# Longer input rows, a second state buffer and a new scheduling model in an eight-core hybrid decoder layer

## The chip, the cores and the metric

One Trainium2 chip, all eight cores, each working on its own 1120 token columns (1056 of a prompt, of which 32 are only history, and 64 of 16 sample sequences). The metric is the device time of the slowest core in microseconds (us). Some executions of these kernels fall into a slower state, in which the cores of one die show a lower granted clock: in a run of the changed kernel of 2220.78 us cores 4 to 7 had 0.818 to 0.819, the other four 0.988 to 0.991. Such runs are left out. I call a run undisturbed when all eight cores show a clock of 0.98 or more; this also leaves out some runs in which only a pair of cores was at 0.97 and about 20 us late.

## The reference, cut to what matters

```python
h = rmsnorm(x, norm_g); z = h @ w_in                 # one projection, split in 7 parts
u_a, gate_a, glu_val, glu_gate, gate_b, q, gate_c = jnp.split(z, splits, axis=-1)
o_a, new_pool = pool_mix(u_a, pool_state, ...)       # windowed means, x silu(gate_a)
a = glu_val * jax.nn.sigmoid(glu_gate)
o_b, new_conv = conv_module(a, conv_state, ...)      # depthwise conv of width 31, LayerNorm, swish, pointwise
o_c = memory_attention(q, mem_k, mem_v)              # 4 heads, 256 memory tokens, x silu(gate_c)
y = rmsnorm(x + concat([o_a, o_b, o_c]) @ w_out)     # returned with the new states
```

## The kernel before

The program is generated by Python code that keeps a model of every engine's time and orders the instructions by it. Weights come through a ring of nine units of 128x1024 in bf16 (GpSimd issues their loads). A projection block is 32 x 3 matmuls on four units; it accumulates in Z0 or Z1.

Start-up: x is loaded in pairs of tiles into three buffers, scaled into HT (bf16) and squared for the norm, while three blocks are accumulated.

```python
xT_d = din("xT", [32, 128, NT])                      # rows of 1120 f32, 4480 bytes
def x_load(a):
    S.dma("sp", ... out=XS[a % 3], in_=xT_d[2 * a:2 * a + 2].rearrange("b p n -> p b n") ...)
for a in range(16):
    act(... SQ2[a % 2] = Square(x_) ...)
    for i in range(2):
        dve(... HT[:, 2 * a + i, :] = x_[:, i, :] * g ...)
    if a:
        dve(... ACC += SQ2[a % 2] ...)
    if a + 3 < 16: x_load(a + 3)
    # ... 18 matmuls per pair; release(6, [HTk[27]]) after tile 27: six more weight units are issued
```

The sample sequences' convolution state of a block of 128 channels lies in ESA, a single buffer. A block's values are written into it, the convolution reads it, it is stored, and the next block's state is loaded.

```python
def v_mult(j, z, zb):
    flush_conv(conv_done, j - 2)
    flush_conv(conv_sampled, j - 1)                  # ESA of the block before is read and stored
    dve(... EA[b] = vp * sg ...)
    dve(... ESA[:, :, 30:34] = vs * sg ...)          # waits for the load; frees Z
```

Small steps of the attention (memory K/V units, scores, softmax, values) wait in a queue and are slipped between the units of the projections when the model says that their inputs are ready; `drain` forces those that are left at a deadline.

```python
def act(fn, n, r=(), w=(), wa=()):
    S.op("act", fn, r=r, w=w, wa=wa, cost=0.25 + n * 0.00084)
def slip():
    units = 0
    while small:
        _, r, w, run, need, un = small[0]
        if (need is not None and need not in given) or S.when("pe", r, w, 0.0) > S.t["pe"] - SLACK:
            break
        if un:
            if units == UNITS_AT_ONCE:
                break
            units += 1
        small.popleft(); run()
def gc_first(h):
    if h: drain(("p", h - 1))                        # values of head h-1 must be done
    gc_block(2 * h)
```

Of the kernel before, what the change touches and what calls it, by code (L numbers as in the profile page):

```python
# [15 lines left out]
D = 4096  # L16
# [7 lines left out]
PACE = 1.7  # L24
SLACK = 1.8
# [142 lines left out]
def build_program(loads=None):  # L168
# [8 lines left out]
    xT_d = din("xT", [32, 128, NT])  # L177
# [25 lines left out]
    with contextlib.ExitStack() as st:  # L203
# [91 lines left out]
        def act(fn, n, r=(), w=(), wa=()):  # L295
            S.op("act", fn, r=r, w=w, wa=wa, cost=0.25 + n * 0.00084)
# [13 lines left out]
        def slip():  # L310
            units = 0
            while small:
                _, r, w, run, need, un = small[0]
                if (need is not None and need not in given) or S.when("pe", r, w, 0.0) > S.t["pe"] - SLACK:
                    break
                if un:
                    if units == UNITS_AT_ONCE:
                        break
                    units += 1
                small.popleft()  # L320
                run()
# [39 lines left out]
        gets = [0]  # L361

        def unit(*key):
            k = gets[0]
            gets[0] += 1
            if recording:
# [6 lines left out]
        def release(n=1, after=()):  # L373
            stream["get"] += n
            fill(after)
# [9 lines left out]
        XS = [CCF[:, i * 2240:(i + 1) * 2240].rearrange("p (b n) -> p b n", b=2) for i in range(3)]  # L385
# [9 lines left out]
        def x_load(a):  # L395
            S.dma("sp", lambda e: e.dma_start(
                out=XS[a % 3], in_=xT_d[2 * a:2 * a + 2].rearrange("b p n -> p b n")), w=[XSb[a % 3]], kb=1120)

        for a in range(3):
            x_load(a)  # L400
        S.dma("act", lambda e: e.dma_start(out=ESA[:, :, :].rearrange("p a b -> p (a b)"), in_=sc_d[0]), w=[ESAb], kb=272)
# [8 lines left out]
        for a in range(16):  # L410
            x_, xb = XS[a % 3], XSb[a % 3]
            if a == 0:
# [3 lines left out]
            for i in range(2):  # L416
                kc = 2 * a + i
                dve(lambda e: e.tensor_scalar(out=HT[:, kc, :], in0=x_[:, i, :], scalar1=col(C_G + kc), scalar2=None,  # L418
                                              op0=ALU.mult), 560, r=[xb, CSb], w=[HTk[kc]])
            if a:  # L420
                dve(lambda e: e.tensor_tensor(out=ACC, in0=ACC, in1=SQ2[a % 2], op=ALU.add), 2240, r=[ACCb, SQ2b[a % 2]], w=[ACCb])  # L421
            if a + 3 < 16:
                x_load(a + 3)
            for i in range(2):
# [40 lines left out]
        act(lambda e: e.copy(out=SG[1][:, 1024:NT], in_=Z[0][:, 1120:1216]), 96, r=[Zb[0]], w=[SGb[1]])  # L465
        A0 = ACC[:, 0, :]
# [9 lines left out]
        def rb_sum(si):  # L476
# [4 lines left out]
                r=[mb], wa=[RBb])  # L481
# [49 lines left out]
        def win(s0, ns):  # L531
            base = ESA[:, s0:s0 + ns, :]
            return bass.AP(tensor=base.tensor, offset=base.offset, ap=[list(base.ap[0]), [34, ns], [1, 4], [1, 31]])

        def esa_load(j):
            S.dma("sp", lambda e: e.dma_start(out=ESA[:, :, :].rearrange("p a b -> p (a b)"), in_=sc_d[j]), w=[ESAb], kb=272)
# [8 lines left out]
        def push_conv(j):  # L545
# [3 lines left out]
            tmp = Y1[:, 0:992].rearrange("p (a t k) -> p a t k", a=8, t=4)  # L549

            def sampled():
                S.dma("act", lambda e: e.dma_start(out=css_d[j], in_=ESA[:, :, :].rearrange("p a b -> p (a b)")), r=[ESAb], kb=272)
                conv_sampled[0] = j
                if j + 1 < 12:
                    esa_load(j + 1)

            for s0 in (0, 8):
                piece(lambda e, s0=s0: e.tensor_tensor(
                    out=tmp, in0=win(s0, 8), in1=CS[:, wc:wc + 31][:, None, None, :].broadcast_to([128, 8, 4, 31]), op=ALU.mult),
                    992, r=[ESAb, CSb], w=[Y1b])  # L560
# [34 lines left out]
        def sigmoid_gate(sg, sgb):  # L595

            dve(lambda e: e.tensor_tensor(out=sg[:], in0=sg[:], in1=RB[:], op=ALU.mult), NT, r=[sgb, RBb], w=[sgb])
            act(lambda e: e.activation(out=sg[:], in_=sg[:], func=AF.Sigmoid), NT, r=[sgb], w=[sgb])
            dve(lambda e: e.tensor_tensor(out=sg[:], in0=sg[:], in1=RB[:], op=ALU.mult), NT, r=[sgb, RBb], w=[sgb])

        def gg_block(j):
# [3 lines left out]
            act(lambda e: e.activation(out=sg[:], in_=sg[:], func=AF.Sigmoid), NT, r=[sgb], w=[sgb])  # L605
            dve(lambda e: e.tensor_tensor(out=sg[:], in0=sg[:], in1=RB[:], op=ALU.mult), NT, r=[sgb, RBb], w=[sgb])

        def v_mult(j, z, zb):
# [3 lines left out]
            flush_conv(conv_sampled, j - 1)  # L612
# [764 lines left out]
```

## Time and profile before

| | before |
|---|---|
| time, median (all 15 runs of the first comparison) | 1911.7 us |
| TensorE busy on the slowest core | 1804.7 of 1908.7 us |
| start-up, until the block after it begins (mean of 8 cores) | 92.8 us |
| from there to the sum of the memory norm | 69.7 us |
| attention, gates, convolutions, to the pointwise stage | 788.7 us |
| the rest | 954.7 us |

The four stages are cut at instructions: the first matmul that waits for the copy of SG out of Z; the one-column matmuls PM<-ONES,PBT; the first multiply CC<-Z,SG on VectorE. In a view of waits the columns are the waiting engine and line, its releaser, the time in total, the times, the longest; in a timeline the start, the duration, engine, line, operation, and in brackets the idle time before it and its releaser. In the names, Z and PM are the accumulators of TensorE, HT the scaled input, SG, CC, G and EA work buffers on chip, RB the token norm, PBT the softmax's values, ring the weight units. In the kernel before L755 copies attention values out of PM, L733 writes the softmax, L803 multiplies memory values by their gate. "Cold" is said of matmuls at a low granted clock, "warm" of those at 1.00.

### The profile page before, as it was taken

How to read it: one execution, taken by the hardware profiler on the slowest of the kernel's cores; microseconds unless marked ns; L12 is line 12 of the kernel's file. 1: busy time of each engine (PE TensorE's matmuls, PEld its weight loads, DVE VectorE, ACT ScalarE, POOL GpSimd, SP SyncE). 2: the span in 40 equal slices, each digit the busy share in tenths (PEclk: the TensorE clock that was granted, in tenths of full speed). 3: DMA queues.
4: the chain of work that ended last, by engine and by line, in shares of the span. 5: the costliest groups of instructions: out<-in, count | busy, mean ns of one | idle time of the engine just before them, and what ended most of it. 6: DMA issues, size and time to landing. Idle time of an engine off the chain costs nothing.

```text
span 1908.7 us, 30037 instructions; the slowest of 8 cores (1901.3 to 1908.7 us)
## 1 busy us (share of the span) xinstructions
PE 1804.7 (95%) x11896; PEld 898.1 (47%) x11896; DVE 1045.5 (55%) x1056; ACT 295.4 (15%) x380; POOL 336.9 (18%) x630
## 2 busy tenths in 40 slices
PE   4799999999999999899999999999999999999991
PEld 2344454544445544455444444444444444444461
DVE  4878989877999998864622222333311111111168
ACT  2542141301113111151400000000000000000010
POOL 1112222122112211222111111111121111111121
PEclk9999999999999999999999999999999999999996
DMA  9986978789757754677375545454687556555559
GB/s 242 260 169 101 159 128 133 126 130 159 136 84 120 115 95 81 101 121 113 61 137 89 84 77 83 77 83 77 103 142 155 116 107 120 107 106 108 106 163 319
DMA packets 129066, 238.28 MB, mean 125 GB/s; under 512 B 19008, under 2 KB 39968, under 8 KB 128416
## 3 DMA queue, kind: packets, MB, share of 16 engines
q0 software_dynamic: 87680, 158.31, 54.5%
q1 hardware_dynamic: 33184, 68.88, 10.9%
q10 hardware_dynamic: 8064, 9.18, 1.4%
q8 instruction: 96, 1.57, 0.3%
q14 instruction: 42, 0.34, 0.1%
HBM read 357.47 MB, written 31.54 MB: 204 GB/s over the span
## 4 chain that ended last, share of the span: by engine, by line
PE 75%; DVE 9%; issue 7%; DMA 5%; ACT 3%; DVEq 0%; ACTq 0%; SPq 0%; POOL 0%; POOLq 0%
PE Z L299 72%; PE PM L299 4%; DMA CC<-xT 3%; DVE CC L572 2%; DMA ring<-w_in 1%; DVE Y L576 1%; ACT PM L728 1%; DVE HT L1201 1%; ACT CC L415 1%; DVE CC L561 0%; DVE SM L723 0%; ACT L728 0%; DVE CC L1201 0%; DVE G L781 0%; DVE SG L781 0%
## 5 line engine op out<-in xcount | busy, mean ns | idle before, releaser
L299 PE MATMUL Z<-HT,ring 128*128 128x512 bf16 (+1 forms) x7232 | 1158.2, 320 | 46.6 <-DVE HT L418 32.0
L299 PEld LDWEIGHTS Z<-HT,ring 128*128 128x128 bf16 x7232 | 562.5, 98 | 629.8 <-issue 70.8
L299 PE MATMUL Z<-CC,ring 128*128 128x512 bf16 (+4 forms) x3336 | 513.6, 317 | 1.9 <-DVE QS L1140 1.7
L299 PEld LDWEIGHTS Z<-CC,ring 128*128 128x128 bf16 x3336 | 254.2, 98 | 260.3 <-issue 2.5
L359 POOL DMA_DIRECT2D ring<-w_in x304 | 162.1, 535 | 778.1 <-PE Z L299 644.4
L572 DVE SCALAR_TENSOR_TENSOR CC<-EA,CS,CC 128x1024 f32<-128x1024 f32 x180 | 230.0, 1278 | 0.3 <-DVE RM L674 0.3
L576 DVE SCALAR_TENSOR_TENSOR Y<-EA,CS,Y 128x1024 f32<-128x1024 f32 x168 | 214.6, 1277 | 0.0
L359 POOL DMA_DIRECT2D ring<-w_out x121 | 64.0, 529 | 382.6 <-PE Z L299 363.8
L1140 DVE TENSOR_TENSOR HT<-Z,EA 128x1088 f32<-128x1088 f32 x16 | 20.7, 1292 | 172.4 <-PE Z L299 172.4
L1022 DVE TENSOR_TENSOR EA<-Z,RB 128x1056 f32<-128x1056 f32 x12 | 15.1, 1258 | 118.0 <-PE Z L299 118.0
L299 PE MATMUL PM<-ring,CC 128*128 128x512 bf16 x256 | 59.7, 379 | 0.0
L781 DVE TENSOR_TENSOR G<-Z,RB 128x1088 f32<-128x1088 f32 x16 | 20.5, 1283 | 63.7 <-PE Z L299 63.7
L1144 DVE TENSOR_TENSOR SS<-SS,SG 128x1088 f32<-128x1088 f32 x27 | 34.9, 1293 | 37.0 <-ACT SG L1142 37.0
L1142 ACT ACTIVATE SG<-HT 128x1088 f32<-128x1088 f32 x16 | 17.8, 1111 | 218.1 <-DVE HT L1140 218.1
L782 ACT ACTIVATE SG<-SG 128x1088 f32<-128x1088 f32 x8 | 8.9, 1112 | 261.6 <-DVE SG L781 261.6
L781 DVE TENSOR_TENSOR SG<-Z,RB 128x1088 f32<-128x1088 f32 x8 | 10.3, 1292 | 69.8 <-PE Z L299 69.8
L782 ACT ACTIVATE G<-G 128x1088 f32<-128x1088 f32 x16 | 17.8, 1111 | 195.8 <-DVE G L781 195.7
L421 DVE TENSOR_TENSOR CC<-CC 128x2240 f32<-128x2240 f32 x15 | 37.3, 2487 | 5.0 <-ACT CC L415 5.0
L415 ACT ACTIVATE CC<-CC 128x2240 f32<-128x2240 f32 x15 | 31.1, 2073 | 41.3 <-DMA CC<-xT 38.6
L299 PEld LDWEIGHTS PM<-ring,CC 128*128 128x128 bf16 x256 | 23.4, 98 | 27.0
L418 DVE TENSOR_SCALAR HT<-CC,CS 128x1120 bf16<-128x1120 f32 x32 | 24.2, 798 | 19.2 <-DMA CC<-xT 19.1
L782 ACT ACT_TABLE_LOAD x13 | 16.7, 1283 | 110.6 <-DVE G L781 66.5
(185 smaller groups left out, 987.9 us busy)
## 6 DMA issues: line engine op xcount, KB each, us to landing
ring<-w_in POOLq DMA_DIRECT2D x304, 256.0 KB, 4.8
ring<-w_out POOLq DMA_DIRECT2D x121, 256.0 KB, 3.9
CC<-xT SPq DMA_DIRECT2D x16, 1120.0 KB, 11.5
EA<-xT SPq DMA_DIRECT2D x28, 544.0 KB, 4.6
ring<-w_mem_k POOLq DMA_DIRECT2D x32, 256.0 KB, 5.9
ring<-w_mem_v POOLq DMA_DIRECT2D x32, 256.0 KB, 6.1
ring<-ckT POOLq DMA_DIRECT2D x32, 256.0 KB, 5.2
ring<-cvP POOLq DMA_DIRECT2D x32, 256.0 KB, 4.9
```

The costliest lines, as they stand in the source:

```text
L299: S.op("pe", lambda e: e.matmul(out, lhsT=lhsT, rhs=rhs, start=start, stop=stop, skip_group_check=skip), r=r, w=w, inc=inc, cost=max(0.05, ...
L359: S.dma("pool", lambda e: e.dma_start(out=RING[s][:, 0:n], in_=src), r=after, w=[RINGb[s]])
L415: act(lambda e: e.activation(out=SQ2[a % 2], in_=x_, func=AF.Square), 2240, r=[xb], w=[SQ2b[a % 2]])
L418: dve(lambda e: e.tensor_scalar(out=HT[:, kc, :], in0=x_[:, i, :], scalar1=col(C_G + kc), scalar2=None, op0=ALU.mult), 560, r=[xb, CSb], w ...
L421: dve(lambda e: e.tensor_tensor(out=ACC, in0=ACC, in1=SQ2[a % 2], op=ALU.add), 2240, r=[ACCb, SQ2b[a % 2]], w=[ACCb])
L572: piece(lambda e, k=k: e.scalar_tensor_tensor(out=YB[j][:, 0:NP_], in0=EA[b][:, 2 + k:2 + k + NP_], scalar=col(wc + k), in1=YB[j][:, 0:NP_ ...
L576: piece(lambda e, k=k: e.scalar_tensor_tensor(out=Y1[:, 0:NP_], in0=EA[b][:, 2 + k:2 + k + NP_], scalar=col(wc + k), in1=Y1[:, 0:NP_], op0 ...
L728: act(lambda e: e.activation(out=m[0:rows, t * 256:(t + 1) * 256], in_=m[0:rows, t * 256:(t + 1) * 256], func=AF.Exp, scale=1.0 / 16, bias ...
L781: dve(lambda e: e.tensor_tensor(out=g[:, 0:W], in0=z[:, 0:W], in1=RB[:, 32:NT], op=ALU.mult), W, r=[zb, RBb], w=gb)
L782: act(lambda e: e.activation(out=g[:, 0:W], in_=g[:, 0:W], func=AF.Silu), W, r=gb, w=gb)
L1140: dve(lambda e: e.tensor_tensor(out=yv, in0=z[:, 0:W], in1=XR[db % 2][:], op=ALU.add), W, r=[zb, XRb[db % 2]], w=[yb])
L1144: dve(lambda e: e.tensor_tensor(out=SY[:], in0=SY[:], in1=SQo[:, 0:W], op=ALU.add), W, r=[SYb, SQob], w=[SYb])
```

## The change

Its intent: load x faster, share the start-up's work with ScalarE, take the wait for the one ESA buffer away at the first block, and let the scheduling model know of table loads and of the supply of weights.

```diff
+UNIT_US = 1.85
-    xT_d = din("xT", [32, 128, NT])
+    xT_d = din("xT", [16, 128, 2 * NT])             # one row of 8960 bytes per pair
+        def act(fn, n, r=(), w=(), wa=(), tab=None):
+            load = tab is not None and tab != table[0]
+            if load:
+                table[0] = tab
+            S.op("act", ..., cost=0.25 + n * 0.00084 + (1.3 if load else 0.0))
 def slip():
-    ... S.when("pe", r, w, 0.0) > S.t["pe"] - SLACK:
+    ... S.when("pe", r, w, 0.0) > S.t["pe"] - (1.2 if small[0][0] == ("rb",) else SLACK):
-                    if units == UNITS_AT_ONCE:
+                    if units == UNITS_AT_ONCE or landed[gets[0] + 1] > S.t["pe"] - 0.5:
 def unit(*key):
+            S.t["pe"] = max(S.t["pe"], landed[k])
 def release(n=1, after=()):
+            for _ in range(n):
+                landed.append(max(landed[-1], S.t["pe"] + 2.2) + UNIT_US)
 for a in range(16):
+            dve(... HT[:, 2 * a, :] = x_[:, 0, :] * g ...)
+            act(... HT[:, 2 * a + 1, :] = Copy(x_[:, 1, :], scale=g) ...)
+            if a > 1:
+                x_sum(a - 1)                        # the sum, one pair later
             act(... Square ...)
-            (both scalings and the sum on VectorE)
+            if a == 13:
+                esa_load(0)                         # was issued at the start
+                esa_load(1)                         # into G[0]
+        def esa(j): G[0] for j == 1, otherwise ESA
-            flush_conv(conv_sampled, j - 1)
+            flush_conv(conv_sampled, j - 1 if j > 2 else j - 2)
 def gc_first(h):
+            else:
+                flush_conv(conv_sampled, 1)
-    ... qs[3] + sp_[3:4] + gs[2] + sp_[4:5] + gs[3]
+    ... qs[3] + gs[2] + sp_[3:5] + gs[3]
 # cut: tab="..." at the calls with a table function, the later reads of xT, the host's layout of xT
```

More of the change, by code (lines that the diff above doesn't have):

```diff
@@ L293, in dve @@
             dve_raw(fn, n, r, w, wa)
-        def act(fn, n, r=(), w=(), wa=()):
-            S.op("act", fn, r=r, w=w, wa=wa, cost=0.25 + n * 0.00084)
+        table = [None]
+        def act(fn, n, r=(), w=(), wa=(), tab=None):
+            load = tab is not None and tab != table[0]
+            if load:
+                table[0] = tab
+            S.op("act", fn, r=r, w=w, wa=wa, cost=0.25 + n * 0.00084 + (1.3 if load else 0.0))
         def mm(out, lhsT, rhs, start, stop, n, r, w, inc=True, skip=False):
@@ L313, in slip @@
                 _, r, w, run, need, un = small[0]
-                if (need is not None and need not in given) or S.when("pe", r, w, 0.0) > S.t["pe"] - SLACK:
+                if (need is not None and need not in given) or S.when("pe", r, w, 0.0) > S.t["pe"] - (1.2 if small[0][0] == ("rb",) else SLACK):
                     break
                 if un:
-                    if units == UNITS_AT_ONCE:
+                    if units == UNITS_AT_ONCE or landed[gets[0] + 1] > S.t["pe"] - 0.5:
                         break
@@ L361, in build_program @@
         gets = [0]
+        landed = [0.0] * NRING
         def unit(*key):
@@ L384, in build_program @@
         fill()
-        XS = [CCF[:, i * 2240:(i + 1) * 2240].rearrange("p (b n) -> p b n", b=2) for i in range(3)]
+        XSF = [CCF[:, i * 2240:(i + 1) * 2240] for i in range(3)]
+        XS = [t.rearrange("p (b n) -> p b n", b=2) for t in XSF]
         XSb = [Buf("XS%d" % i) for i in range(3)]
@@ L395, in x_load, with x_sum, esa, esa_load @@
         def x_load(a):
-            S.dma("sp", lambda e: e.dma_start(
-                out=XS[a % 3], in_=xT_d[2 * a:2 * a + 2].rearrange("b p n -> p b n")), w=[XSb[a % 3]], kb=1120)
+            S.dma("sp", lambda e: e.dma_start(out=XSF[a % 3], in_=xT_d[a]), w=[XSb[a % 3]], kb=1120)
+        def x_sum(a):
+            dve(lambda e: e.tensor_tensor(out=ACC, in0=ACC, in1=SQ2[a % 2], op=ALU.add), 2240, r=[ACCb, SQ2b[a % 2]], w=[ACCb])
+        def esa(j):
+            if j == 1:
+                return G[0][:, 0:544].rearrange("p (s r) -> p s r", s=16), G[0][:, 0:544], Gb[0]
+            return ESA[:, :, :], ESA[:, :, :].rearrange("p a b -> p (a b)"), ESAb
+        def esa_load(j):
+            _, t, tb = esa(j)
+            S.dma("sp", lambda e: e.dma_start(out=t, in_=sc_d[j]), w=[tb], kb=272)
         for a in range(3):
             x_load(a)
-        S.dma("act", lambda e: e.dma_start(out=ESA[:, :, :].rearrange("p a b -> p (a b)"), in_=sc_d[0]), w=[ESAb], kb=272)
         act(lambda e: e.copy(out=IDB[:], in_=IDF[:]), 128, r=[IDb], wa=[IDb])
@@ L411, in build_program @@
             x_, xb = XS[a % 3], XSb[a % 3]
+            dve(lambda e: e.tensor_scalar(out=HT[:, 2 * a, :], in0=x_[:, 0, :], scalar1=col(C_G + 2 * a), scalar2=None,
+                                          op0=ALU.mult), 560, r=[xb, CSb], w=[HTk[2 * a]])
+            act(lambda e: e.activation(out=HT[:, 2 * a + 1, :], in_=x_[:, 1, :], func=AF.Copy, scale=col(C_G + 2 * a + 1)), NT,
+                r=[xb, CSb], w=[HTk[2 * a + 1]])
+            if a > 1:
+                x_sum(a - 1)
             if a == 0:
@@ L415, in build_program @@
                 act(lambda e: e.activation(out=SQ2[a % 2], in_=x_, func=AF.Square), 2240, r=[xb], w=[SQ2b[a % 2]])
-            for i in range(2):
-                kc = 2 * a + i
-                dve(lambda e: e.tensor_scalar(out=HT[:, kc, :], in0=x_[:, i, :], scalar1=col(C_G + kc), scalar2=None,
-                                              op0=ALU.mult), 560, r=[xb, CSb], w=[HTk[kc]])
-            if a:
-                dve(lambda e: e.tensor_tensor(out=ACC, in0=ACC, in1=SQ2[a % 2], op=ALU.add), 2240, r=[ACCb, SQ2b[a % 2]], w=[ACCb])
             if a + 3 < 16:
                 x_load(a + 3)
+            if a == 13:
+                esa_load(0)
+                esa_load(1)
             for i in range(2):
@@ L465, in build_program @@
         act(lambda e: e.copy(out=SG[1][:, 1024:NT], in_=Z[0][:, 1120:1216]), 96, r=[Zb[0]], w=[SGb[1]])
+        x_sum(15)
         A0 = ACC[:, 0, :]
@@ L480, in rb_sum @@
             act(lambda e: e.activation(out=RB[:, c0:c1], in_=m[:, 0:c1 - c0], func=AF.Sqrt, scale=1.0 / D, bias=EPS), c1 - c0,
-                r=[mb], wa=[RBb])
+                r=[mb], wa=[RBb], tab="sqrt")
             recip(RB[:, c0:c1], c1 - c0, RBb)
@@ L529, in flush_conv, with win @@
                 convq.popleft()[1]()
-        def win(s0, ns):
-            base = ESA[:, s0:s0 + ns, :]
+        def win(j, s0, ns):
+            base = esa(j)[0][:, s0:s0 + ns, :]
             return bass.AP(tensor=base.tensor, offset=base.offset, ap=[list(base.ap[0]), [34, ns], [1, 4], [1, 31]])
-        def esa_load(j):
-            S.dma("sp", lambda e: e.dma_start(out=ESA[:, :, :].rearrange("p a b -> p (a b)"), in_=sc_d[j]), w=[ESAb], kb=272)
         def piece(fn, n, r=(), w=(), wa=(), after=None, first=False):
@@ L549, in push_conv @@
             tmp = Y1[:, 0:992].rearrange("p (a t k) -> p a t k", a=8, t=4)
+            _, es, esb = esa(j)
             def sampled():
-                S.dma("act", lambda e: e.dma_start(out=css_d[j], in_=ESA[:, :, :].rearrange("p a b -> p (a b)")), r=[ESAb], kb=272)
+                S.dma("act", lambda e: e.dma_start(out=css_d[j], in_=es), r=[esb], kb=272)
                 conv_sampled[0] = j
-                if j + 1 < 12:
-                    esa_load(j + 1)
+                nxt = 2 if j == 0 else j + 1
+                if j != 1 and nxt < 12:
+                    esa_load(nxt)
             for s0 in (0, 8):
                 piece(lambda e, s0=s0: e.tensor_tensor(
-                    out=tmp, in0=win(s0, 8), in1=CS[:, wc:wc + 31][:, None, None, :].broadcast_to([128, 8, 4, 31]), op=ALU.mult),
-                    992, r=[ESAb, CSb], w=[Y1b])
+                    out=tmp, in0=win(j, s0, 8), in1=CS[:, wc:wc + 31][:, None, None, :].broadcast_to([128, 8, 4, 31]), op=ALU.mult),
+                    992, r=[esb, CSb], w=[Y1b])
                 piece(lambda e, s0=s0: e.tensor_reduce(
@@ L597, in sigmoid_gate @@
             dve(lambda e: e.tensor_tensor(out=sg[:], in0=sg[:], in1=RB[:], op=ALU.mult), NT, r=[sgb, RBb], w=[sgb])
-            act(lambda e: e.activation(out=sg[:], in_=sg[:], func=AF.Sigmoid), NT, r=[sgb], w=[sgb])
+            act(lambda e: e.activation(out=sg[:], in_=sg[:], func=AF.Sigmoid), NT, r=[sgb], w=[sgb], tab="sig")
             dve(lambda e: e.tensor_tensor(out=sg[:], in0=sg[:], in1=RB[:], op=ALU.mult), NT, r=[sgb, RBb], w=[sgb])
@@ L604, in gg_block @@
             dve(lambda e: e.tensor_tensor(out=sg[:], in0=z[:, 0:NT], in1=RB[:], op=ALU.mult), NT, r=[zb, RBb], w=[sgb])
-            act(lambda e: e.activation(out=sg[:], in_=sg[:], func=AF.Sigmoid), NT, r=[sgb], w=[sgb])
+            act(lambda e: e.activation(out=sg[:], in_=sg[:], func=AF.Sigmoid), NT, r=[sgb], w=[sgb], tab="sig")
             dve(lambda e: e.tensor_tensor(out=sg[:], in0=sg[:], in1=RB[:], op=ALU.mult), NT, r=[sgb, RBb], w=[sgb])
@@ L611, in v_mult @@
             flush_conv(conv_done, j - 2)
-            flush_conv(conv_sampled, j - 1)
+            flush_conv(conv_sampled, j - 1 if j > 2 else j - 2)
+            ev, _, evb = esa(j)
             if z is None:
-                vp, vs, vb = EA[b][:, 0:1056], ESA[:, :, 30:34], [EAb[b], ESAb]
+                vp, vs, vb = EA[b][:, 0:1056], ev[:, :, 30:34], [EAb[b], evb]
             else:
@@ L618, in v_mult @@
                 r=vb + [sgb], w=[EAb[b]])
-            dve(lambda e: e.tensor_tensor(out=ESA[:, :, 30:34], in0=vs, in1=sg[:, 1056:NT].rearrange("p (s r) -> p s r", s=16),
-                                          op=ALU.mult), 64, r=vb + [sgb], wa=[ESAb])
+            dve(lambda e: e.tensor_tensor(out=ev[:, :, 30:34], in0=vs, in1=sg[:, 1056:NT].rearrange("p (s r) -> p s r", s=16),
+                                          op=ALU.mult), 64, r=vb + [sgb], wa=[evb])
             S.dma("act", lambda e: e.dma_start(out=csp_d[j], in_=EA[b][:, 1026:1056]), r=[EAb[b]], kb=16)
@@ L672, in mem_sum @@
                        [IDb, PBb[0]], [PMb[1]], inc=(i == 1))
-            act(lambda e: e.activation(out=RM[:, 0:2], in_=PM[1][:, 0:2], func=AF.Sqrt, scale=1.0 / D, bias=EPS), 2, r=[PMb[1]], w=[RMb])
+            act(lambda e: e.activation(out=RM[:, 0:2], in_=PM[1][:, 0:2], func=AF.Sqrt, scale=1.0 / D, bias=EPS), 2, r=[PMb[1]], w=[RMb], tab="sqrt")
             dve(lambda e: e.reciprocal(out=RM[:, 0:2], in_=RM[:, 0:2]), 12, r=[RMb], wa=[RMb])
@@ L729, in softmax @@
                                            scale=1.0 / 16, bias=sm[0:rows, 4 + t:5 + t], accum_out=sm[0:rows, 8 + t:9 + t]), 256,
-                    r=[mb, smb], wa=[mb, smb])
+                    r=[mb, smb], wa=[mb, smb], tab="exp")
             dve(lambda e: e.reciprocal(out=sm[0:rows, 12:12 + ng], in_=sm[0:rows, 8:8 + ng]), 12, r=[smb], wa=[smb])
@@ L781, in gate @@
             dve(lambda e: e.tensor_tensor(out=g[:, 0:W], in0=z[:, 0:W], in1=RB[:, 32:NT], op=ALU.mult), W, r=[zb, RBb], w=gb)
-            act(lambda e: e.activation(out=g[:, 0:W], in_=g[:, 0:W], func=AF.Silu), W, r=gb, w=gb)
+            act(lambda e: e.activation(out=g[:, 0:W], in_=g[:, 0:W], func=AF.Silu), W, r=gb, w=gb, tab="silu")
         def gc_block(c):
@@ L910, in ln_stat @@
                 r=[PMb[1], ESAb], wa=[QSb])
-            act(lambda e: e.activation(out=va, in_=va, func=AF.Sqrt, scale=1.0, bias=EPS), n, r=[QSb], wa=[QSb])
+            act(lambda e: e.activation(out=va, in_=va, func=AF.Sqrt, scale=1.0, bias=EPS), n, r=[QSb], wa=[QSb], tab="sqrt")
             recip(va, n, QSb)
@@ L921, in swish @@
                     act(lambda e: e.activation(out=CC[:, 2 * j, :], in_=YB[j], func=AF.Silu, scale=col(C_LNG + j), bias=col(C_LNB + j)),
-                        W, r=[yb[0], CSb], w=yb)
+                        W, r=[yb[0], CSb], w=yb, tab="silu")
                 piece(lambda e, j=j: e.tensor_tensor(out=YB[j], in0=YB[j], in1=SS[:], op=ALU.subtract), W, r=[SSb, yb[0]], w=yb)
@@ L936, in build_program @@
         sp_ = [lambda i=i: gb_spill(i) for i in range(5)]
-        others.extend(qs[0] + qs[1] + gs[0] + sp_[0:1] + qs[2] + sp_[1:2] + gs[1] + sp_[2:3] + qs[3] + sp_[3:4] + gs[2] + sp_[4:5] + gs[3])
+        others.extend(qs[0] + qs[1] + gs[0] + sp_[0:1] + qs[2] + sp_[1:2] + gs[1] + sp_[2:3] + qs[3] + gs[2] + sp_[3:5] + gs[3])
         others.extend(lambda dj=dj: gb_block(dj) for dj in range(7))
@@ L1127, in xr_load @@
             if db < NFULL:
-                S.dma("sp", lambda e: e.dma_start(out=XR[db % 2][:], in_=xT_d[db][:, 32:NT]), w=[XRb[db % 2]], kb=544)
+                S.dma("sp", lambda e: e.dma_start(out=XR[db % 2][:], in_=xT_d[db // 2][:, (db % 2) * NT + 32:(db % 2 + 1) * NT]), w=[XRb[db % 2]], kb=544)
         xr_load(0)
@@ L1188, in xq_load @@
                 t, tb = XQ[i % 4]
-                S.dma("pool", lambda e: e.dma_start(out=t[:, 0:c1 - c0], in_=xT_d[NFULL + r][:, 32 + c0:32 + c1]), w=[tb],
+                S.dma("pool", lambda e: e.dma_start(out=t[:, 0:c1 - c0], in_=xT_d[(NFULL + r) // 2][:, (r % 2) * NT + 32 + c0:(r % 2) * NT + 32 + c1]), w=[tb],
                       kb=(c1 - c0) / 2)
@@ L1208, in seg_sum @@
             ones_mm(m[:, 0:n], mb, HLs[0][:, 0:n], HLs[1][:, 0:n], HLsb)
-            act(lambda e: e.activation(out=SY[:, c0:c1], in_=m[:, 0:n], func=AF.Sqrt, scale=1.0 / D, bias=EPS), n, r=[mb], wa=[SYs[si]])
+            act(lambda e: e.activation(out=SY[:, c0:c1], in_=m[:, 0:n], func=AF.Sqrt, scale=1.0 / D, bias=EPS), n, r=[mb], wa=[SYs[si]], tab="sqrt")
             recip(SY[:, c0:c1], n, SYs[si])
@@ L1334, in _host_inputs @@
         m = dict(shared)
-        m.update({"xT": np.ascontiguousarray(x.T).reshape(32, 128, NT), "memT": memT[b],
+        m.update({"xT": np.ascontiguousarray(x.T.reshape(16, 2, 128, NT).transpose(0, 2, 1, 3)).reshape(16, 128, 2 * NT), "memT": memT[b],
                   "ckT": np.ascontiguousarray(ckc).reshape(4, 8, 128, 1024),
```

## The prediction

Passages that told of the hardware what no trace of this case shows are cut out of the prediction, and the cuts are marked. Its sum came to 24 us: 7.5 for parts 1 to 3, 6.5 for the second buffer, 10 for the scheduling model. The 7.5 is the 9.3 us of parts 1 to 3 less 1.8 us that I took off for a limit of the memory (HBM) and for waits for weights, an estimate of mine that no trace shows. The 331 GB/s are read in 20 to 40 us of core 3; what limit they should be held against is not shown, so the rival that the memory limits the start-up has little for it. The 1.28 us are a load of a function table on ScalarE.

> **What bounds the kernel now**
>
> I read the table of cores first. All eight lie between 1901 and 1909 us at clocks of 0.984 to 0.988, so the profiled run is an undisturbed one (1909.74 us), and one core (core 3) can stand for all. Then the page: busy time and slices.
>
> ```profile
> PE 1804.7 (95%) x11896; PEld 898.1 (47%) x11896; DVE 1045.5 (55%) x1056; ACT 295.4 (15%) x380; POOL 336.9 (18%) x630
> PE   4799999999999999899999999999999999999991
> DMA  9986978789757754677375545454687556555559
> ```
>
> TensorE is busy 95% of the span. The change leaves its matmuls alone, so it can only win what TensorE loses: 104 us of idle time plus time at a low clock. The windows say where the idle lies: 58 - 29.3 = 28.7 us before 58, 7.4 us in 58 to 90, 4 us around 125, 9 us in 280 to 420, 8.7 us in 420 to 830, 39 us after 1860, little elsewhere. The tail and the pure matmul stages are not touched. Next, who TensorE waited for:
>
> ```profile
> PE Z L299 <- DVE HT L418: 32.0, 13, 13.5
> PE Z L299 <- DMA ring<-w_in: 6.6, 4, 4.8
> PE PM L299 <- ACT CC L755: 6.2, 7, 1.5
> PE Z L299 <- DVE ESA L619: 4.1, 1, 4.1
> ...
> PE PM L752 <- ACT PBT L733: 3.4, 2, 3.1
> PE PM L299 <- DVE CC L803: 2.8, 2, 1.4
> ```
>
> The first line is the start-up (x loaded, scaled into HT, three blocks accumulated meanwhile). VectorE is named because it writes HT, but its own timeline shows two regimes: until about 58 us it waits for x, after that it never rests, and a pair of x tiles takes 3.83 us:
>
> ```profile
> 38.93 1.52 DVE L418 TENSOR_SCALAR HT<-CC,CS 128x1120 bf16<-128x1120 f32 x2 [1.76 <-DMA CC<-xT]
> ...
> 75.31 1.51 DVE L418 TENSOR_SCALAR HT<-CC,CS 128x1120 bf16<-128x1120 f32 x2
> 76.73 2.48 DVE L421 TENSOR_TENSOR CC<-CC 128x2240 f32<-128x2240 f32 x1
> 79.14 1.51 DVE L418 TENSOR_SCALAR HT<-CC,CS 128x1120 bf16<-128x1120 f32 x2
> ```
>
> The DMA queues in three windows, columns packets, MB, share of the 16 engines. First 12 to 20 us (x and weights), then 58 to 66 (x alone), then 100 to 118 (the memory tokens, 8192-byte rows, and weights):
>
> ```profile
> q1 hardware_dynamic: 322, 1.37, 58.8%
> q0 software_dynamic: 322, 0.59, 44.9%
> ```
>
> ```profile
> q1 hardware_dynamic: 544, 2.30, 98.0%
> ```
>
> ```profile
> q0 software_dynamic: 721, 1.31, 50.4%
> q1 hardware_dynamic: 398, 2.87, 48.4%
> ```
>
> So the engines are full from 2 us to the end of the loads even with x alone, at only 288 GB/s, and x and the weights take turns one packet each. Loads of x landed about 6.6 us apart while weights came too (12.5, 19.4, 25.9, 32.5, 39.0), about 3.8 us apart later.
>
> After start-up:
>
> ```profile
> 128.04 36.67 PE L299 MATMUL Z<-HT,ring 128*128 128x512 bf16 x216 [4.12 <-DVE ESA L619]
> ...
> 396.30 0.26 PE L752 MATMUL PM<-IDB,PBT 64*128 64x64 bf16 x2 [3.10 <-ACT PBT L733]
> ...
> 802.86 5.33 PE L299 MATMUL Z<-HT,ring 128*128 128x512 bf16 x24 [4.84 <-DMA ring<-w_in]
> ```
>
> The chain behind the first: ESA's store issued at 118.43, its next load at 123.89, landed by 127.57, then the multiply that frees Z. The third follows a burst of eight units drained together at 796.3, which emptied the weight ring.
>
> [...]
>
> - [...] 322 packets against 322. Longer x packets thus win a larger share against the weights.
> - [...] 3.81 MB of x and 1.41 MB of weights, which are read at twice that size as f32, are 6.63 MB in 20 us, 331 GB/s. [...]
> - [...] after the 4.12 us gap the granted clock is 0.58 in 126 to 130 and 0.57 in 130 to 134, then 1.00. [...]
> - [...] The trace shows 1.28 us; the old scheduling model charged none.
>
> **The change part by part**
>
> *1. x in rows of 8960 bytes instead of two of 4480.* From 58 to 66 us: 2.30 MB are 513 packets of 4480 bytes, 0.98 x 8 us x 16 / 513 = 244 ns each. From 100 to 118 us, 350 packets of 8192 bytes took 0.484 x 18 x 16 / 350 = 398 ns each. The slope is 154 ns per 3712 bytes, the fixed part about 58 ns; an 8960-byte packet is then estimated at 430 ns against 488 for two. Each engine carries 128 fewer packets: 128 x 58 ns = 7.4 us. Since the engines are full all along, that comes off the landing of the last x tile (84.9 us)[...]. Taking turns with a weight packet of 189 ns, a load of x needs 8 x (430 + 189) = 4.95 us instead of 16 x (244 + 189) = 6.9. The first nine weight units are 81 packets per engine and now last to about 2 + 81 x 0.62 = 52 us; the set for tile 16 is wanted at about 48, so TensorE waits for weights there, but has time to catch up (2.8 us of work per pair against 3.4 to 5 of loading).
>
> *2. The first ESA load moves behind the x loads.* 8 packets per engine, about 1 us off the start. In return the six weight units released after tile 27 come earlier against the last load and take turns with its 8 packets: 8 x 189 ns = 1.5 us, of which about 0.5 was paid before. The two cancel.
>
> *3. ScalarE scales every second HT tile; the sum is put off by one pair.* VectorE falls from 3.83 to 0.72 + 2.40 = 3.1 us a pair, ScalarE rises to 1.1 + 2.07 = 3.2. Both lie below the 3.44 us of a load (8 x 430 ns), so the DMA alone paces the end. VectorE lagged the landings by 1.9 us (84.91 landed, 86.79 scaled); that lag goes. Parts 1 to 3: 7.4 + 1.9 = 9.3 us at most. [...]
>
> *4. A second buffer (G0) for ESA of block 1.* The multiply needs neither store nor load. It can run after the gate's last multiply (ends 120.98): 1.25 + 0.23, done at 122.5 in today's times, 1.4 us before TensorE asks (123.92). The 4.1 us go, and the cold stretch, 5.4 us at 0.57 to 0.58, gives about 2.4 more: 6.5. G0 is first wanted at 246.8 and the conv pieces that read it end at 198, so the added flush costs nothing.
>
> *5. The scheduling model.* It now charges 1.3 us per table load, models when a weight unit lands, and takes a small unit only if the next weight will be there; two spilled gates move between the third and fourth group of memory gates, so the units drained at 796 can slip in earlier. At stake after 140 us: ring 5.3, L755 6.2, L733 3.4, L803 2.8, and some 3 us at a low clock (24 matmuls took 5.33 and 5.43 us where 3.85 is usual): about 20. The two long waits are what is modelled; I expect both gone (8 us and 3 of clock), a third of the short ones saved, and about 4 us returned as new waits from slower draining: 10 us net.
>
> Sum: 7.5 + 6.5 + 10 = 24 us, 1910.5 - 24 = 1886.5.
>
> **Rivals**
>
> - *The start is limited by HBM, not per packet.* For it: the mixed stage already reads 331 GB/s. Against: x alone ran at 288 with full engines. Then only the 1.9 us lag and little else is won: about 1892.
> - *ScalarE becomes the pace.* 3.2 us a pair plus waits is close to 3.44, and it now frees a buffer 3.2 us after a landing instead of 2.1. With two loads still in flight I think it hidden; otherwise 1 to 3 us are lost.
> - *Slower pacing collects units that must be drained at the deadlines.* It would show as bursts and new ring waits; part 5 gives 0 to 3: about 1894.
> - *Everything works and small waits vanish too:* 9.3 + 7 + 18 = 34 us, 1876.
>
> **Range and chances**
>
> A gain over 2% means under 1872.3, thus 38 us, more than the sum of all upper ends (9.3 + 7 + 20 = 36): 5%. Slower by 2% would need a broken schedule: 1%. The parts are nearly independent, with errors of some 3, 1.5 and 5 us; I widen that to a range of 1876 to 1898.
>
> **What the profile will show**
>
> Right, if: x loads in packets of 8960 bytes at about 430 ns, the last landing at 77 to 79 us and the matmuls after start-up beginning at 83 to 86 (before: 92.2); VectorE waiting for x up to the end; no wait on ESA near 118 and full clock there; no wait of TensorE over 2 us between 140 and 1000; later stages as before, shifted. Wrong, if: x packets take 480 ns or more, ScalarE has no gaps from 50 to 80 us, or waits for the ring or new drains appear. Matmuls and the tail from 1860 should cost the same; a shift there would mean that I missed something.

## The result, and the profile after

The changed kernel took 1877.98 us in the median of 11 runs against 1911.7. The ratio is 0.9825 (95% interval 0.9815 to 0.9834). It is the mean time of one kernel's runs over that of the other's of the same rounds, so not quite the ratio of the medians. Executions in which one die ran at a lower clock are left out of the means. The gain of 33.7 us lies in the predicted range and within 2%, but near the lower end of the range (1876 to 1898 us): 24 us were expected.

| mean of 8 cores, us | start-up | to the memory norm | attention and conv | rest | end |
|---|---|---|---|---|---|
| before | 92.8 | 69.7 | 788.7 | 954.7 | 1905.8 |
| after | 87.1 | 64.7 | 766.5 | 953.9 | 1872.2 |
| difference | -5.7 | -5.0 | -22.2 | -0.8 | -33.6 |

The page of the changed kernel, busy time and slices of TensorE:

```profile
PE 1796.6 (96%) x11896; PEld 897.1 (48%) x11896; DVE 1036.0 (55%) x1040; ACT 312.4 (17%) x395; POOL 336.8 (18%) x630
PE   4799999999999999999999999999999999999991
```

The matmuls are the same and take 8 us less busy time, so less of it was at a low clock; the one slice with an 8 is gone. Who TensorE waited for (slowest core, core 3 as before):

```profile
PE Z L306 <- DMA ring<-w_in: 22.4, 5, 14.8
PE PM L306 <- DMA ring<-w_in: 6.9, 3, 4.4
PE Z L306 <- DVE HT L437: 6.9, 6, 2.0
PE PM L306 <- DVE SG L1296: 3.7, 1, 3.7
```

The waits on the evacuations by ScalarE (L755, L733), on CC L803 and on ESA have no counterpart. The waits for the ring grew, but all of that growth lies in start-up (25.1 us of the 29.3; after 100 us they are 4.3, against 5.3 before), where they stand for what was called a wait for HT before: TensorE now has x before it has weights. Its timeline shows this, and where the start-up ends (92.21 in the kernel before):

```profile
14.85 1.09 PE L306 MATMUL Z<-HT,ring 128*128 128x512 bf16 x3 [14.85 <-DMA ring<-w_in]
...
24.74 1.01 PE L306 MATMUL PM<-HT,ring 128*128 128x512 bf16 x2 [4.40 <-DMA ring<-w_in]
...
87.22 7.75 PE L306 MATMUL Z<-HT,ring 128*128 128x512 bf16 x48 [1.47 <-ACT SG L493]
```

The DMA queues of the changed kernel in 12 to 20 us (x and weights):

```profile
q1 hardware_dynamic: 217, 1.69, 69.9%
q0 software_dynamic: 223, 0.40, 31.5%
```

Still one packet each, but x now gets 1.69 MB in this stretch instead of 1.37, and the weights 0.40 instead of 0.59. In 66 to 74 us x is nearly alone:

```profile
q1 hardware_dynamic: 308, 2.47, 93.7%
```

These 2.47 MB are 276 packets of 8960 bytes (the other 32 packets have 4 bytes and take about 9 ns), which took 0.937 x 8 x 16 / 276 = 435 ns each. The prediction set an estimated 430 ns against 2 x 244 ns, measured in one window of core 3. The packet records of all cores, over the whole loading of x, say less: 437 ns in the mean for a long packet, and 230 ns for a short one, so 460 ns for two. The other half of the comparison was off, not the estimate.

Around the former ESA wait, windows of TensorE (busy time, count, granted clock, DMA share, GB/s), before:

```profile
126.00:130.00 4.00, 1.96 (x7) 0.58 0.64 112
130.00:134.00 4.00, 4.00 (x17) 0.57 0.00 0
```

and after:

```profile
118.00:122.00 4.00, 4.00 (x28) 1.00 0.40 58
122.00:126.00 4.00, 4.00 (x28) 1.00 0.66 92
126.00:130.00 4.00, 4.00 (x28) 1.00 0.78 211
130.00:134.00 4.00, 4.00 (x28) 1.00 0.90 184
```

There is no gap, so there are no cold matmuls after it: 28 matmuls in each 4 us, against 7 and 17. (The changed kernel is 5 us earlier here, so the place of the old wait lies in the first two windows.)

### The profile page after: what moved, and what is told of

Its sections match the earlier page's. It is cut to its first block, busy times and chain, and to the rows that moved or that the text cites. A ratio compares the mean times of both kernels' runs of the same rounds, so it can differ in the third digit from the quotient of the medians.

```text
span 1876.8 us, 30032 instructions; the slowest of 8 cores (1868.5 to 1876.8 us)
## 1 busy us (share of the span) xinstructions
PE 1796.6 (96%) x11896; PEld 897.1 (48%) x11896; DVE 1036.0 (55%) x1040; ACT 312.4 (17%) x395; POOL 336.8 (18%) x630
## 4 chain that ended last, share of the span: by engine, by line
PE 90%; DMA 5%; DVE 3%; ACT 1%; issue 1%; DVEq 0%; SPq 0%; POOL 0%; ACTq 0%; POOLq 0%
PE Z L306 86%; PE PM L306 4%; DMA CC<-xT 3%; DMA ring<-w_in 1%; DVE HT L1232 1%; DVE CC L1232 0%; ACT CC L446 0%; DVE G L810 0%; DVE SG L810 0%; PE PM L781 0%; DVE SS L489 0%; DVE G L1232 0%; ACT CC L444 0%; ACT HT L439 0%; DVE QS L1171 0%
## 5 line engine op out<-in xcount | busy, mean ns | idle before, releaser
L367 POOL DMA_DIRECT2D ring<-cvP x32 | 17.0, 530 | 83.8 <-PE Z L306 34.5
L367 POOL DMA_DIRECT2D ring<-ckT x32 | 17.4, 545 | 75.9 <-PE PM L306 45.6
```

The source lines that it names most:

```text
L367: S.dma("pool", lambda e: e.dma_start(out=RING[s][:, 0:n], in_=src), r=after, w=[RINGb[s]])
```

## The experiments

The question left by the result: which parts carry the 22 us of the third stage, of which I had expected 10, and why start-up gave less. My theory was that the parts add up. The rivals were that the scheduling gains come from the other parts shifting the program against its small steps, and that within the scheduling part a single piece does it. Every kernel here gave correct results. The first four ran on a chip on which a pair of cores often lagged, in runs of the kernel before too, so their ratios are blurred; I compare undisturbed runs and the stages. The stages are of the profiled run of each kernel, the time is the median of its undisturbed runs.

| kernel | time, us | start-up | to memory norm | attention, conv | ratio to before (95%) |
|---|---|---|---|---|---|
| after (first set) | 1877.3 | 87.1 | 64.7 | 766.5 | 0.9825 (0.9815-0.9834) |
| s_none | 1902.0 | 88.1 | 64.7 | 789.3 | 0.9917 (0.9876-0.9958) |
| b_sched | 1887.3 | 92.9 | 71.3 | 769.9 | 0.9863 (0.9807-0.9919) |
| e_one | 1883.7 | 87.9 | 72.4 | 769.7 | 0.9855 (0.9778-0.9932) |
| s_table | 1896.9 | 87.4 | 64.7 | 785.9 | 0.9951 (0.9882-1.0021) |
| s_landed | 1878.9 | 87.5 | 64.7 | 766.7 | 0.9850 (0.9815-0.9886) |
| s_order | 1885.2 | 87.1 | 64.7 | 772.7 | 0.9859 (0.9846-0.9871) |
| x_rows | 1881.8 | 90.6 | 64.7 | 765.8 | 0.9860 (0.9831-0.9888) |
| x_split | 1879.4 | 88.3 | 64.7 | 767.8 | 0.9830 (0.9817-0.9842) |
| after_again | 1877.3 | 87.1 | 64.7 | 766.8 | 0.9820 (0.9808-0.9833) |
| x_xs4 | 1875.7 | 86.4 | 64.7 | 766.2 | 0.9814 (0.9802-0.9827) |
| x_xs4_late | 1876.3 | 86.8 | 64.7 | 766.3 | 0.9816 (0.9804-0.9829) |
| best | 1887.7 | 86.8 | 64.7 | 785.4 | 0.9877 (0.9860-0.9894) |

In the profiles of b_sched, e_one and best, cores 6 and 7 lagged and lift the means of the second and third stage; without those two, e_one's second stage is 70.5 and b_sched's 69.5, b_sched's third is 765.9, and best's third is 776.0 to 780.6 on each core. Six kernels share the start-up of the changed one, instruction for instruction (after, after_again, s_none, s_table, s_landed, s_order): their start-up reads 87.1 to 88.1, so a difference of less than about 1 us in that column shows nothing. The medians of e_one and best rest on two executions each, that of s_table on three, the others on four or more.

### s_none: all of the scheduling part undone

```diff
-cost=0.25 + n * 0.00084 + (1.3 if load else 0.0)
+cost=0.25 + n * 0.00084
-(1.2 if small[0][0] == ("rb",) else SLACK)
+SLACK
- or landed[gets[0] + 1] > S.t["pe"] - 0.5
-            S.t["pe"] = max(S.t["pe"], landed[k])
-qs[3] + gs[2] + sp_[3:5] + gs[3]
+qs[3] + sp_[3:4] + gs[2] + sp_[4:5] + gs[3]
```

> The changed kernel with the whole scheduling part undone (no charge for table loads, no model of landing weights, old place of the spilled gates, old slack), start-up and second ESA buffer kept. My theory: the scheduling part is worth about 20 us, as the difference of the traces leaves after 5.0 us of start-up and 7 us around the ESA wait: about 1897 us, and waits of TensorE on L755/L733 and one long wait for the weight ring are back. Rival: much of those 20 us comes from everything being shifted by the other parts, which moves small steps against the units; then 1885 to 1890 us.

Measured: 1902.0 us, +24.7. The third stage is back at 789.3 (before: 788.7), the second stays at 64.7. So the third stage's 22 us are the scheduling part, and the second stage's 5 us do not need it. The rival of a mere shift falls.

### b_sched: the scheduling part alone, in the kernel before

The same edits and the table names, added to the kernel before.

> The kernel before with the scheduling part alone. My theory (parts add up): 1911 - 20 = 1891 us, start-up unchanged (matmuls after it begin at about 92 us), the 4.1 us ESA wait still there. Rival (the model only fits the new start-up): under 10 us won, 1901 us or more.

Measured: 1887.3 us, 24 less than before, with the old start-up (92.9) and the ESA wait (3.45 us on core 1). Done alone or undone alone, the part is worth the same, so it adds up with the others. The part has four pieces. Three are undone one by one below; the fourth, the smaller slack for the step of the token norm (`rb`), was never undone alone. That step lies in the second stage, which reads 64.7 with it and without it (s_none).

### e_one: one ESA buffer

```diff
-            if j == 1:                    # in esa(j)
+            if j == -1:
-                esa_load(1)
-                nxt = 2 if j == 0 else j + 1
-                if j != 1 and nxt < 12:
+                nxt = j + 1
+                if nxt < 12:
-flush_conv(conv_sampled, j - 1 if j > 2 else j - 2)
+flush_conv(conv_sampled, j - 1)
-            else:
-                flush_conv(conv_sampled, 1)
```

> The changed kernel with one ESA buffer again (block 1 waits for store and load). My theory: the wait of about 4 us on ESA and a half-clock stretch of about 5 us return, 1877.5 + 6.5 = 1884 us. Rival: the wait is back but the clock does not fall, +4 us, 1881.5; or the lost time is made up later, +0 to 2 us.

Measured: 1882.6 and 1884.8 us in the two undisturbed runs, +6.4 in the mean. The timeline of TensorE on core 1:

```profile
121.73 35.02 PE L306 MATMUL Z<-HT,ring 128*128 128x512 bf16 x216 [3.37 <-DVE ESA L647]
```

The wait is back, and the 216 matmuls after it took 35.0 us. The same group took 36.67 us on core 3 of the kernel before; warm it takes 33.2 us (in the changed kernel 360 matmuls in 55.67 us on core 1, of which the first 144 take 22.49). So on these two cores the gap costs itself and 1.8 to 3.5 us of cold matmuls. My theory holds. How low the clock falls and how long it stays low differs between cores: in the kernel before the eight waits on ESA are 2.6 to 4.1 us and the 216 matmuls take from 33.3 us (warm) to 36.7. The traces show no length of wait from which on the clock falls: after 2.85 us (core 1 of the kernel before) it was 0.74 in 126 to 130 us and 0.83 in 130 to 134, after 2.92 us (core 0) 1.00 in both, after 4.12 us (core 3) 0.58 and 0.57. The "half-clock stretch" of my expectation is this last one.

### s_table: no charge for table loads

```diff
-cost=0.25 + n * 0.00084 + (1.3 if load else 0.0)
+cost=0.25 + n * 0.00084
```

> The changed kernel without the charge of 1.3 us per table load in the scheduling model, the rest kept. My theory: this charge is what removed the waits on ScalarE (9.6 us in the kernel before, and about 2 us of clock): +6 to +11 us, 1884 to 1889 us, with L755/L733 waits back. Rival: the model of landing weights alone spaces the small steps out enough, so the waits do not come back: within 2 us of 1877.5.

Measured: 1896.9 us, +19.6, twice what I expected. Waits of TensorE on core 1, 155 to 960 us:

```profile
PE PM L781 <- ACT PBT L762: 5.6, 3, 3.4
PE PM L306 <- ACT CC L784: 4.9, 7, 1.6
PE PM L306 <- DVE CC L832: 3.5, 2, 2.1
PE PM L306 <- DVE CC L842: 1.2, 3, 0.8
```

The waits on ScalarE are back, and those on VectorE's multiplies of memory values too, which I had not put down to the table charge. On this core the changed kernel waits for nothing in that span. One line of code that only adds to a number in the model carries most of the gain: without it the model takes a ScalarE step that begins with a table load to be 1.3 us shorter than it is, and TensorE stands before the steps that depend on it (10.5 us in the first two lines above). The load in the timeline of core 3 of the kernel before:

```profile
111.53 1.28 ACT L598 ACT_TABLE_LOAD   x1 [2.43 <-DVE SG L597]
112.83 1.14 ACT L598 ACTIVATE SG<-SG 128x1120 f32<-128x1120 f32 x1
```

ScalarE was idle here; the multiply that it waited for ended at 111.46 us, and the sigmoid began 1.3 us after the start of the load. It is no longer when ScalarE has just worked: the loads at 208.85 and 827.54 us begin 0.01 to 0.02 us after the instruction before them and take 1.28, and the next one follows 0.01 to 0.02 us later. One rival is open: a margin of another kind, a larger SLACK or a flat charge on every ScalarE step, was not tried, so it is not shown that the charge had to fall on the table loads.

### s_landed: no model of landing weights

```diff
- or landed[gets[0] + 1] > S.t["pe"] - 0.5
-            S.t["pe"] = max(S.t["pe"], landed[k])
```

> The changed kernel without the model of landing weight units (the pacing and TensorE's modelled wait for a unit taken out), table charge and new order kept. The runs before: the scheduling part is worth about 24 us (1901 without it, 1887 with it alone in the kernel before), and taking out the table charge alone cost 19. Theory A (table charge nearly alone): at most +5 us, 1877 to 1882. Theory B (the pieces only work together: without pacing the ring runs dry): +8 us or more, with waits for the ring of 4 us or more after 140 us.

Measured: 1878.9 us; third stage 766.7 against 766.5. The pacing is worth nothing that I can resolve. The ring waits of the kernel before (2.5 to 7.2 us a core in this stage) did not end because of it: without it they are 0 to 4.1 us, with it 0 to 4.3.

### s_order: spilled gates at their old places

> The changed kernel with the spilled gates at their old places. Theory A (the new place lets the units slip in that were drained in one burst): the burst of eight units before the last memory gate returns, with a ring wait of 4 to 5 us and a cold stretch: +6 us, 1883. Theory B (the pacing and the charge alone already avoid the burst): within 2 us of 1877.

The edit is the last two lines of s_none's. Measured: 1885.2 us, third stage +6.2. Timeline of TensorE on core 3:

```profile
768.67 1.75 PE L306 MATMUL PM<-CC,ring 128*128 128x4 bf16 x64
776.51 5.85 PE L306 MATMUL Z<-HT,ring 128*128 128x512 bf16 x24 [6.09 <-DMA ring<-w_in]
```

The burst of eight units (64 matmuls of 4 columns) is there again, the ring runs dry, and the next unit runs cold (5.85 us instead of 3.85). In the changed kernel one more projection block lies before the deadline, and the units go in between. The pieces overlap: 19.4 (charge) + 6.2 (order) + 0.2 (pacing) is 25.8, a little over the 22.8 that they are worth together.

### x_rows: rows of 4480 bytes

```diff
-xT_d = din("xT", [16, 128, 2 * NT])
+xT_d = din("xT", [32, 128, NT])
-out=XSF[a % 3], in_=xT_d[a]
+out=XS[a % 3], in_=xT_d[2 * a:2 * a + 2].rearrange("b p n -> p b n")
 # and the later reads and the host's layout, as before
```

> The changed kernel with x in rows of 4480 bytes again. My theory: packets go back from about 450 to 2 x 244 ns, so about 3 us of loading time return (last landing near 85 us): 1880 to 1881 us. Rival: loading in the changed kernel is limited by other things (buffers freed later by ScalarE, weights against the last load), so rows do not matter: within 1 us of 1877. Second rival: short rows help the weights in the taking of turns, so it gets even faster.

Measured: 1881.8 us, start-up +3.5. My theory holds, and the rows are the larger half of the start-up's gain. The last x lands at 84.8 us in the mean of the cores, against 81.3 in the changed kernel and 84.4 in the kernel before. The short packets took 234 ns in the mean, less than the 244 that I had put in.

### x_split: VectorE scales both tiles

```diff
-            dve(... HT[:, 2 * a, :] ...)
-            act(... HT[:, 2 * a + 1, :] ...)
+            for i in range(2):
+                dve(... HT[:, 2 * a + i, :] ...)
```

> The changed kernel with VectorE scaling both x tiles of a pair again (sum still put off by one pair). My theory: VectorE needs 3.83 us a pair again, behind the loads from about 66 us on, where x alone lands every 3.1 to 3.2 us: up to 2 us lost at the end of start-up, 1879. Rival: ScalarE, at 3.2 us a pair without a gap from 71 to 80 us, holds the buffers of x and starves the DMA engines for about 1.5 us; giving its work back to VectorE frees it: same time or up to 1 us faster.

Measured: 1879.4 us, start-up +1.2, little over the spread of 1 us; the ratios (0.9817 to 0.9842 against 0.9815 to 0.9834) do not separate the two. Steadier is the time from the landing of the last x to the block after start-up: 6.9 us here, 5.5 to 6.1 in the six kernels with the changed start-up, 8.4 in the kernel before. So the lag of VectorE is back in part, 1 us of it. The other 1.5 us stay won; the sum is still put off by a pair here, and no run takes that out. ScalarE in the changed kernel near the end of the loads (core 3):

```profile
74.08 1.22 ACT L439 ACTIVATE HT<-CC,CS 128x1120 bf16<-128x1120 f32 x1
75.20 2.06 ACT L446 ACTIVATE CC<-CC 128x2240 f32<-128x2240 f32 x1
77.28 1.23 ACT L439 ACTIVATE HT<-CC,CS 128x1120 bf16<-128x1120 f32 x1
```

It works without a pause, and a buffer of x is free for the next load only after its square. Windows 74 to 78 us of the changed kernel (busy time of PE, PEld, DVE, ACT, POOL, each with its count, then clock, DMA share, GB/s):

```profile
74.00:76.00 2.00, 2.00 (x14) 0.93 (x13) 2.00 (x3) 2.00 (x3) 0.05 (x1) 1.00 0.74 299
76.00:78.00 2.00, 2.00 (x14) 0.92 (x12) 2.00 (x2) 1.98 (x2) 1.93 (x4) 1.00 0.71 224
```

and of x_split, core 3 too:

```profile
74.00:76.00 2.00, 1.05 (x8) 0.41 (x7) 1.96 (x4) 1.24 (x1) 0.00 (x0) 1.00 0.92 309
76.00:78.00 2.00, 2.00 (x14) 1.03 (x13) 2.00 (x1) 0.83 (x1) 1.43 (x3) 1.00 1.01 411
```

The DMA share falls to 0.7 where ScalarE holds the buffers, and not where it has less to do; in the mean of the cores it is 0.88 and 0.94 over these 4 us. So the rival sees the starved DMA engines rightly, but it costs little: the last x lands no earlier in x_split (81.4 us, against 81.3 in the changed kernel and 81.5 in its repeat).

### after_again, x_xs4, x_xs4_late: more buffers, later weights

> The changed kernel once more, as the measure for the three that run with it on the same chip: 1876 to 1878 us in its fast runs.

Measured: 1877.3 us; the measure is steady.

```diff
-XSF = [CCF[:, i * 2240:(i + 1) * 2240] for i in range(3)]
+XSF = [CCF[:, i * 2240:(i + 1) * 2240] for i in (0, 1, 2, 6)]
-(a % 3, a + 3)
+(a % 4, a + 4)
```

> The changed kernel with four buffers for x instead of three. My theory: the DMA engines, busy only 0.74 and 0.71 in 74 to 76 and 76 to 78 us because ScalarE frees the buffers late, stay full, and the last load lands about 1.5 us earlier: 1875.5 us. Rival: the weights released for the next block take the place that becomes free, and the first weights come even later: no gain.

Measured: the DMA share in 74 to 76 and 76 to 78 us is now 0.96 and 0.98 on core 3, as intended, but start-up is only 0.7 us shorter in the mean, less than the spread of 1 us, and the intervals of the ratios (0.9802 to 0.9827 against 0.9808 to 0.9833) overlap. Not resolved; at most 1 us.

```diff
-                elif kc == 27:
-                    release(6, [HTk[27]])
+                elif kc == 29:
+                    release(6, [HTk[29]])
```

> Four buffers for x, and the six weight units that are released after tile 27 released after tile 29. My theory: the last load of x no longer takes turns with them (its interval falls from 4.5 us to about 3.5): 1 us more than with four buffers alone, 1874.5 us. Rival: the weights then come too late for the block after start-up, and the microsecond is lost there in a wait for the ring.

Measured: 1876.3 us, start-up 86.8. No gain over x_xs4, no loss for the block after it. Neither version is shown to beat the changed kernel.

### best: a slower modelled supply on top

The label was given in hope. The edit to x_xs4_late is `UNIT_US = 2.1` instead of 1.85.

> The last one, and in the scheduling model 2.1 us per landing unit instead of 1.85. The changed kernel still waits 4.3 us for the ring after 140 us in three places, with a cold stretch behind the first. My theory: a slower modelled supply spaces small units further, and these waits shrink by half: 1872 us. Rival: the slower pacing collects units that are then drained in a burst before a deadline: 1876 us or more.

Measured: 1886.6 and 1888.7 us undisturbed, 10 slower than the changed kernel. The ring waits did not shrink: on core 3 they fell from 4.3 to 0.3 us after 90 us, but in the mean of the cores they are 1.2 us against 1.4. VectorE first and then TensorE show another wait (core 3):

```profile
386.58 0.23 DVE L648 TENSOR_TENSOR ESA<-Z,SG 128x64 f32<-128x64 f32 x1 [6.69 <-DMA ESA<-scT]
```

```profile
390.39 0.26 PE L781 MATMUL PM<-IDB,PBT 64*128 64x64 bf16 x2 [9.29 <-ACT PBT L762]
```

With the small steps later, the softmax's maximum falls behind the ESA multiply in VectorE's order, that multiply waits 6.7 us for its load, and TensorE waits 9.3 us for the softmax. Every core has this wait, of 9.0 to 11.1 us. The rival was right that slower pacing loses, but not by an empty ring: by a chain through the one ESA buffer.

## Why the prediction was right or wrong

It was right in the time's range and in most mechanisms, but not in its sum, which was short by 9.7 us: the scheduling term was 12 us too small, the terms of start-up and of the second buffer together 3 us too large. The range held because it was wider than the errors given for the parts (3, 1.5 and 5 us); that the total came so near its lower end was not foreseen.

- **Rows (part 1), 7.4 us at most.** Longer rows did load faster, and the estimate for a long packet was good: 430 ns, measured 437 over all x loads of all cores. What was too large is the time of the short packet beside it: 244 ns is one window of core 3, where the other cores show 214 to 242; over the whole loading it is 230. So two short ones cost 460 ns, not 488, and 128 x (460 - 437) ns = 2.9 us are won, not 7.4. That is what the loads show: the last x landed 3.1 us earlier in the mean of the cores (84.4 to 81.3), and putting the short rows back costs 3.5 us (x_rows). On core 3 the last x was used at 81.8 us, not landed at 77 to 79, and the block after start-up began at 87.2, not 83 to 86. Nor is a fixed cost of 58 ns in every packet shown: the median long packet took 351 ns, two median short ones 346 (all cores together), so the gain lies among the slower packets. Why these cost less with long rows is open.
- **Taking turns.** As said: one packet each (217 of x against 223 of weights in 12 to 20 us, core 3), loads of x landing 4.6 to 6.1 us apart while weights come too (core 3), TensorE now waiting for weights and catching up.
- **ESA load moved (part 2).** Not tried by itself. In the kernel before the 128 packets of this load took 141 ns in the mean on core 3, so 8 of them take 1.1 us of an engine, about the microsecond that was put in.
- **Scaling on ScalarE (part 3), 1.9 us of lag.** From the landing of the last x to the block after start-up it was 8.4 us and is 5.8, so 2.6 us are won, a little more than the lag. About 1 of them is the scaling (x_split); the put-off sum was not undone by itself. The rival "ScalarE becomes the pace" was seen but costs little: on core 3 it was busy for 9.0 of the 10 us before 80, yet the DMA engines were idle for only 1.1 us of the 81 before the last landing (mean of the cores), and x_xs4, which fills them again, wins at most 1 us.
- **Parts 1 to 3 together:** 7.5 predicted, 5.7 measured (3.1 before the last landing, 2.6 after it).
- **Second ESA buffer (part 4), 6.5.** 5.0 in the stage means, about 6.4 in the time when undone, 7.6 on core 3 (4.1 us of wait and 3.5 of cold matmuls). The cause was right. The size was read from core 3, which has the longest wait and the longest cold stretch of the eight: in the mean the wait is 3.2 us and the cold stretch costs 1.8. The table of the cores' spans was not enough to let one core stand for all.
- **Scheduling (part 5), 10 net of a stake of about 20.** This is the term that was mis-sized. Measured: 22.2. The assumption "a third of the short ones saved, and about 4 us returned as new waits" was wrong: on core 1 all 18.8 us of waits in that stage went, and busy time fell by 6.3 us (770.6 to 764.3), which is the low clock behind them. Nothing was given back on that core; on the slowest, 4.3 us of ring waits stand where 5.3 stood. The clock was undervalued too: 3 us expected, 6.3 on core 1. I had spread the credit over the pieces by their names. In fact, undone one at a time, the table charge carries 19.4 us, the place of the spilled gates 6.2, and the model of landing weights, which I took for a main piece, nothing measurable.
- **Rivals.** HBM as the limit of start-up: the rows did help, so it did not rule alone; with long rows, and x nearly alone, 316 GB/s were moved in 66 to 74 us, where 288 was seen with x alone before. What the memory can give at most, and whether it has a part in the slower packets, no run shows. Bursts at deadlines: not seen in this version; the slower pacing of best loses, but by another chain. "Small waits vanish too", 1876, came closest.
- **Marks of being wrong.** Packets of 480 ns or more: no. ScalarE without gaps from 50 to 80 us: only near the end (21.8 of the 30 us busy on core 3). New waits for the ring: none on four cores after 90 us, 2.2 to 4.3 us on the others.
- **Tail and matmul stages.** Unchanged, as said: 953.9 against 954.7 us.

## What to carry to other kernels

Where a program orders its instructions by a model of time, an uncharged fixed cost of about a microsecond can cost far more than itself: here the charge of 1.3 us for a table load was worth 19.6 us (s_table), because steps placed too early stopped TensorE again and again. Long gaps were followed, on most cores, by cold matmuls: after the waits of 2.6 to 4.1 us on ESA in the kernel before the granted clock in 126 to 130 us was 0.50 to 0.74 on six cores and 1.00 on two. Compare modelled and traced times for the engines off the critical path first, and undo one piece at a time to find which carries the gain: here it was the charge, not the pacing written beside it. Giving an idle engine work also makes it an owner of buffers, so look at when it frees them. And size a term on all cores and over the whole stretch: the slowest core in one window gave 244 ns for a packet that took 230, and 6.5 us for a wait that is worth 5.0 in the mean.
